# A decoder block on one core: another order of the seven-product steps in the feed-forward gate/up blocks, with the last one's raw weights split ahead of its sums

## The chip, the core and the metric

The kernel runs on one core of a Trainium2 chip. The metric is the time of one execution in device microseconds (us); less is better. The engines are TensorE (PE in the profile; PEld is its weight load), VectorE (DVE), ScalarE (ACT), GpSimd (POOL) and SyncE (SP), which here only issues DMAs.

## The reference

One layer of a decoder with 256 positions and a width of 2048: a normalised input goes through one wide projection, three groups of dilated window attention and a gated linear recurrence, whose outputs are mixed and added to the input. Then comes the feed-forward part, where the change is:

```python
a = rmsnorm(h, norm_ffn_pre[layer])
gt, up = jnp.split(a @ w_ffn_gate_up[layer], [D_FF], axis=-1)   # 2048 x (2 * 5632)
ff = (jax.nn.silu(gt) * up) @ w_ffn_down[layer]                 # 5632 x 2048
h = h + rmsnorm(ff, norm_ffn_post[layer])
```

All of it is float32.

## The kernel before

**Split numbers.** PE multiplies in a reduced 32-bit format (`F32R`). So each float32 weight tile is split on the fly: ACT copies it to the format (the high half, `w` or `dh`), and DVE subtracts that from the original (the low half, `wl` or `dl`). The activations are split in the same way, once. A product is then three matmuls: high by high, low weight by high activation, high weight by low activation.

**Blocks and steps.** Gate and up are computed in 11 blocks (0 to 10) of 512 gate and 512 up columns. A block has eight steps; a step `(m, kind)` takes rows 256m to 256m + 255 of the weights, as four tiles of 128 x 512. Two sides of 128 positions by two column groups by two row tiles make eight products, 24 matmuls of 512 columns. Kind 0 does just that ("plain"). Kinds 1 and 2 do the step in seven products, 21 matmuls, after a scheme like Strassen's: four of them need sums of weight tiles, and four sums of activations (`h7`). In kind 1 ("own sums") DVE makes the weight sums from the loaded tiles: three additions (`sum`, L476, L482, L483), ahead of the splits. In kind 2 ("fetched") the sums were made much earlier and stored in DRAM (`presum`); two DMAs fetch them (`s`), and only three of the four raw tiles are loaded beside. Either kind splits sums (`w` and `wl`, two halves of 1024 columns each) and three raw tiles (`dh` and `dl`, 1536 columns).

**Order of the products.** In `multiply_wide` a seven-product step takes the products with sums first and those with raw tiles behind, but in the last one of a block (`b.last7`) the raw ones first, so that the result bank `p1` is done early and `gather` can begin. Blocks 2 to 10 have the order `GATE_UP5`, block 1 `GATE_UP3`; in both, the step at place 6 is the block's last seven-product step. I number the places 0 to 7 and say "step 6" for them. In `GATE_UP5` before, the steps 2, 3 and 5 are fetched, 4 and 6 have own sums, and 0, 1 and 7 are plain.

**What sets the order on the engines.** There is no scheduler: each engine gets its instructions in the order in which the Python code issues them. During step i of PE, the code issues the split of step i + 2 (`prepare`), then DMAs on SP's queue: the sums for step i + 4 (`fetch_sums`) and the raw weights for step i + 5, which wait until the raw buffer of step i + 2 is free (three buffers). Between the steps stand the leftovers of the block before: `gather` (L553 to L557) and `complete` (L563) take its banks on DVE, ACT applies silu (L1460), DVE makes the product `e` (L1462). Then `turn_act` turns this product, which needs four DMA transposes on SP: ACT copies the words apart (L1413) behind the split of step 3, SP issues the transposes (L1419), and two steps on ACT copies the result together (L1428, it waits for the transposes) and sends it to DRAM (`acts`, L1430). Buffers for `dh` and `dl` serve two steps, so the split of step i waits until PE is through with that of two seven-product steps ago.

**Sums of activations.** `pair_sums` makes the five `h7` from `hT`, in pieces: at every `yield` the code goes on with other work, and it comes back twice per step.

Of the kernel before, what the change touches and what calls it, by code (L numbers as in the profile page):

```python
# [14 lines left out]
F32 = mybir.dt.float32  # L15
F32R = mybir.dt.float32r
I32 = mybir.dt.int32
U16 = mybir.dt.uint16
AF = mybir.ActivationFunctionType
# [23 lines left out]
    [(2, 0), (3, 0), (0, 1), (4, 0), (1, 1), (5, 0), (6, 0), (7, 0)],  # L43
]
GATE_UP3 = [(3, 0), (4, 0), (0, 2), (5, 0), (1, 1), (6, 0), (2, 2), (7, 0)]
GATE_UP5 = [(5, 0), (6, 0), (0, 2), (2, 2), (1, 1), (4, 2), (3, 1), (7, 0)]
PLACE = (0, 2, 1, 3)
DOWN = [[(m, m in by7) for m in range(KF // 2)] for by7 in (range(4, 20, 3), (2, 4, 7, 10, 13, 16, 18))]

# [53 lines left out]
def tile_hybrid_block(ctx: ExitStack, tc: tile.TileContext, t, out):  # L103
    nc = tc.nc
# [12 lines left out]
    def nm(s):  # L117
        serial[0] += 1
        return f"{s}_{serial[0]}"
# [13 lines left out]
    def p3(s, dtype, n, bufs, tag=None):  # L133
        return wide_pool[-1].tile([P, n], dtype, tag=tag or s, bufs=bufs, name=nm(s))
# [73 lines left out]
    def ptile(s):  # L208
        pool, n = (wide_pool[-1], 2) if wide_pool else (fp[0], 5)
        return pool.tile([P, 512], F32, tag="p", bufs=n, name=nm(s))  # L210
# [9 lines left out]
    blocks, chunks, wides, steps = [], [], [], []  # L220
# [27 lines left out]
    def add_wide_block(*args, **kw):  # L248
        b = Wide(*args, **kw)
        wides.append(b)  # L250
        for i in range(len(b.order)):
            n = len(steps)
            slots.append(lambda n=n: load_wide(n))
            items.append((steps, n, len(slots) - 1))
            steps.append([b, i, None, None])
# [39 lines left out]
    pre, pre_in = {}, {}  # L295
# [104 lines left out]
    def wslot():  # L400
        return stream.tile([P, 2048], F32R, tag="w", bufs=N_SPLIT, name=nm("w"))
# [41 lines left out]
    def split_wide(n):  # L443

        b, i, raw = steps[n][:3]
        m, by7 = b.order[i]
        prep = b.prep(m, by7) if b.prep else iter(())
        next(prep, None)
        if (b, i) == spare:
            hi = p3("spare", F32R, 2048, 1, "sum")  # L450
            lo = Joined(p3("spare", F32R, 1536, 4, "d"), p3("spare", F32R, 512, 4, "d"))
            nc.scalar.activation(hi, raw, AF.Copy)
            for c in (slice(0, 1536), slice(1536, 2048)):
                nc.vector.tensor_sub(lo[:, c], raw[:, c], hi[:, c].bitcast(F32))
            steps[n][3] = hi, lo
            return
        hi, lo = wslot(), p3("wl", F32R, 2048, 3)
        if not by7:
            for c in (slice(0, 1024), slice(1024, 2048)) if b.halves else (slice(0, 2048),):
                nc.scalar.activation(hi[:, c], raw[:, c], AF.Copy)  # L460
                next(prep, None)
                nc.vector.tensor_sub(lo[:, c], raw[:, c], hi[:, c].bitcast(F32))  # L462
            steps[n][3] = hi, lo
            return
        d = raw[:, 512:]
        if by7 == 2:
            for c, x in zip((slice(0, 1024), slice(1024, 2048)), pre_in.pop(n)):
                nc.scalar.activation(hi[:, c], x, AF.Copy)  # L468
                nc.vector.tensor_sub(lo[:, c], x, hi[:, c].bitcast(F32))  # L469
            dhi, dlo = p3("dh", F32R, 1536, 4, "d"), p3("dl", F32R, 1536, 4, "d")  # L470
            nc.scalar.activation(dhi, d, AF.Copy)
            nc.vector.tensor_sub(dlo, d, dhi.bitcast(F32))
            steps[n][3] = hi, lo, dhi, dlo
            return
        s = p3("sum", F32, 2048, 1)
        nc.vector.tensor_add(  # L476
            s[:, :1024].rearrange("p (a c) -> p a c", a=2),
            raw[:, 512:1536].rearrange("p (a c) -> p a c", a=2),
            raw[:, None, :512].to_broadcast([P, 2, 512]),
        )  # L480
        nc.scalar.activation(hi[:, :1024], s[:, :1024], AF.Copy)  # L481
        nc.vector.tensor_add(s[:, 1024:1536], raw[:, 512:1024], s[:, 512:1024])  # L482
        nc.vector.tensor_add(s[:, 1536:], raw[:, 1536:], s[:, 1024:1536])  # L483
        nc.scalar.activation(hi[:, 1024:], s[:, 1024:], AF.Copy)
        next(prep, None)
        dhi, dlo = p3("dh", F32R, 1536, 4, "d"), p3("dl", F32R, 1536, 4, "d")
        nc.scalar.activation(dhi, d, AF.Copy)  # L487
        for c in (slice(0, 1024), slice(1024, 2048)):
            nc.vector.tensor_sub(lo[:, c], s[:, c], hi[:, c].bitcast(F32))  # L489
        next(prep, None)  # L490
        nc.vector.tensor_sub(dlo, d, dhi.bitcast(F32))  # L491
        steps[n][3] = hi, lo, dhi, dlo

    def multiply_wide(n, sides=(0, 1), groups=(0, 1), between=lambda: None):
        b, i = steps[n][:2]
# [69 lines left out]
    def seven_sums(f, dst):  # L565

        s = ptile("s").rearrange("p (n t) -> p n t", n=4)
        a11, a12, a21, a22 = f[:, 0, :P], f[:, 1, :P], f[:, 0, P:], f[:, 1, P:]
        nc.vector.tensor_sub(s[:, 0, :], a22, a21)
        nc.vector.tensor_sub(s[:, 2, :], a11, a21)  # L570
        nc.vector.scalar_tensor_tensor(
            out=s[:, 1, :], in0=s[:, 0, :], scalar=-1.0, in1=a11, op0=OP.mult, op1=OP.subtract
        )
        nc.vector.tensor_add(s[:, 3, :], a12, s[:, 1, :])
        return (
            lambda: nc.scalar.activation(dst[:, 0], s, AF.Copy),
            lambda: nc.vector.tensor_sub(dst[:, 1], s, dst[:, 0].bitcast(F32)),
        )

    def sums_of(dst):  # L580
        return lambda n: (dst[:, 0, n, :], dst[:, 1, n, :])
# [3 lines left out]
    def pair_sums(src, out, slot, pairs=H7):  # L585

        for m in pairs:
            f = ptile("f").rearrange("p (k t) -> p k t", k=2)
            x = src.slots[m]
            nc.vector.tensor_add(f, x[:, :, 0, :].bitcast(F32), x[:, :, 1, :].bitcast(F32))  # L590
            dst = slot().rearrange("p (z n t) -> p z n t", z=2, n=4)
            yield
            for part in seven_sums(f, dst):
                yield
                part()
            out[m] = sums_of(dst)
            yield
# [216 lines left out]
    def more_x(c):  # L814
        if 0 < c < KD // 2 - 1:
            transpose_in(xt, colg, xT, c + 1)
        if c == 2:
            lanes[1].append(pair_sums(xT, x7, lambda: rslot("so")))
# [556 lines left out]
    def more_h(c):  # L1375
        if c + 1 < KD // 2:
            transpose_in(h_t, colg[:, 16:32], hT[0], c + 1)
        if c == 3:
            mix_gain(3, 1, wides[last_mix])
            residual_of(6, (0, 1), False)  # L1380
            residual_of(7, (0, 1), False)
            lanes[0].append(second_norm())
        if c == 4:
            lanes[1].append(pair_sums(hT[0], h7, lambda: rslot("so"), range(5)))
# [203 lines left out]
    def y_sums():  # L1588
        while not {0, 1} <= yT[0].there:
            yield  # L1590
        yield from pair_sums(yT[0], y7, lambda: rslot("so"), (0, 1))
# [27 lines left out]
    for half in range(2):  # L1619
        for g in range(3):  # L1620
            c = 1024 * g + 512 * half
# [28 lines left out]
    for j in range(1, 11):  # L1650
        add_wide_block(w, (512 * j, FF + 512 * j), GATE_UP5 if j > 1 else GATE_UP3, lambda k: hT[0](k),
                       lambda m: h7[m], evac_ffn, j % 2 == 0,
# [23 lines left out]
    for i in range(len(items)):  # L1676
        kind, n, _ = items[i]
        b, c = kind[n][:2]
# [99 lines left out]
```

## Time and profile before

| | before |
|---|---|
| median of 3 runs (lowest, highest) | 1692.96 us (1692.91, 1698.74) |
| the profiled execution | 1695.45 us, span of its instructions 1693.6 us |
| mean granted clock of TensorE | 0.998 |
| ACT: shares of the span, instructions | 59%, 1121 |
| DMA | 445.27 MB, mean 263 GB/s |
| gate/up blocks 1 to 10 | about 1040 to 1452 us of the span |

All times in the profile are counted from the start of the span. A row of the time line gives the start, the length, engine and line, what is written and read, and, in brackets, the idle time of the engine before it with what ended that. Lengths of rows that follow each other overlap by up to 0.1 us, so that the distance of two starts is the better measure of what an instruction costs on a full engine. The windows give the busy time of each engine in a stretch, the number of its instructions, the granted clock (1.00 is full speed), the DMA engines' share and GB/s.

### The profile page before, as it was taken

How to read it: one execution, taken by the hardware profiler on the slowest of the kernel's cores; microseconds unless marked ns; L12 is line 12 of the kernel's file. 1: busy time of each engine (PE TensorE's matmuls, PEld its weight loads, DVE VectorE, ACT ScalarE, POOL GpSimd, SP SyncE). 2: the span in 40 equal slices, each digit the busy share in tenths (PEclk: the TensorE clock that was granted, in tenths of full speed). 3: DMA queues.
4: the chain of work that ended last, by engine and by line, in shares of the span. 5: the costliest groups of instructions: out<-in, count | busy, mean ns of one | idle time of the engine just before them, and what ended most of it. 6: DMA issues, size and time to landing. Idle time of an engine off the chain costs nothing. (4 is left out here: it accounts for less than half of the span.)

```text
span 1693.6 us, 22264 instructions
## 1 busy us (share of the span) xinstructions
PE 1675.1 (99%) x8142; PEld 1401.8 (83%) x8142; DVE 1406.6 (83%) x1593; ACT 997.7 (59%) x1121; POOL 210.0 (12%) x358
## 2 busy tenths in 40 slices
PE   9999999999999999999999999999999999999997
PEld 7888888888888888888888888878888888788886
DVE  6999888866876876876578888999999999889987
ACT  6655555544455545555545557676777777665653
POOL 0012122234433432210000000000000000000000
PEclk9999999999999999999999999999999999999999
DMA  8578888899999999998868656998999999887673
GB/s 288 203 249 283 274 273 274 273 282 272 266 236 252 291 235 259 291 322 284 300 200 286 200 184 196 295 282 282 290 288 293 285 297 294 281 261 276 231 261 130
DMA packets 264640, 445.27 MB, mean 263 GB/s; under 512 B 39073, under 2 KB 105809, under 8 KB 263377
## 3 DMA queue, kind: packets, MB, share of 16 engines
q1 hardware_dynamic: 237936, 375.25, 68.4%
q0 software_dynamic: 17984, 41.97, 12.2%
q10 hardware_dynamic: 8608, 26.62, 4.2%
q8 instruction: 64, 1.05, 0.3%
q14 instruction: 48, 0.39, 0.1%
HBM read 414.41 MB, written 65.54 MB: 283 GB/s over the span
## 5 line engine op out<-in xcount | busy, mean ns | idle before, releaser
L140 PE MATMUL acc<-xT,w 128*128 128x256 f32 (+1 forms) x2048 | 365.1, 338 | 0.0
L140 PEld LDWEIGHTS acc<-xT,w 128*128 128x128 f32 x2048 | 312.0, 188 | 44.7
L462 DVE TENSOR_TENSOR wl<-raw,w 128x2048 fp32r<-128x2048 f32 (+1 forms) x131 | 284.0, 2175 | 62.8 <-ACT w L460 60.8
L407 DVE TENSOR_TENSOR w<-raw,w 128x1024 fp32r<-128x1024 f32 x176 | 215.3, 1223 | 144.0 <-ACT w L406 143.9
L406 ACT ACTIVATE w<-raw 128x1024 fp32r<-128x1024 f32 x176 | 186.1, 1059 | 192.7 <-PE acc L140 143.4
L460 ACT ACTIVATE w<-raw 128x2048 fp32r<-128x2048 f32 (+1 forms) x131 | 237.7, 1821 | 95.2 <-PE acc L140 23.0
L140 PE MATMUL acc<-w,xT 128*128 128x512 f32 x578 | 168.8, 392 | 0.0
L369 POOL COPY beats<-raw 128x1 f32<-128x1 f32 x185 | 103.7, 560 | 507.6 <-DMA raw<-in_w_in 506.7
L481 ACT ACTIVATE w<-sum 128x1024 fp32r<-128x1024 f32 x57 | 60.6, 1063 | 176.4 <-DVE sum L476 169.1
L489 DVE TENSOR_TENSOR wl<-sum,w 128x1024 fp32r<-128x1024 f32 x114 | 137.7, 1221 | 0.6 <-ACT w L481 0.6
L140 PE MATMUL acc<-w,hT 128*128 128x512 f32 x402 | 131.2, 392 | 0.4 <-DVE hT L1305 0.4
L140 PEld LDWEIGHTS acc<-w,xT 128*128 128x128 f32 x578 | 108.2, 188 | 22.2
L140 PE MATMUL aux<-w,xT 128*128 128x512 f32 x344 | 109.8, 389 | 0.0
L491 DVE TENSOR_TENSOR dl<-raw,dh 128x1536 fp32r<-128x1536 f32 x57 | 100.2, 1757 | 6.8 <-ACT dh L487 5.0
L140 PE MATMUL aux<-w,hT 128*128 128x512 f32 x318 | 102.8, 389 | 0.0
L140 PEld LDWEIGHTS acc<-w,hT 128*128 128x128 f32 x402 | 75.4, 188 | 16.3 <-DVE hT L1305 0.9
L140 PE MATMUL acc<-w,so 128*128 128x512 f32 x264 | 88.4, 389 | 0.0
L140 PE MATMUL acc<-w,a 128*128 128x512 f32 x268 | 83.8, 389 | 1.1 <-DVE e L563 1.1
L140 PE MATMUL aux<-w,so 128*128 128x512 f32 x252 | 84.4, 389 | 0.0
L487 ACT ACTIVATE dh<-raw 128x1536 fp32r<-128x1536 f32 x57 | 84.1, 1475 | 0.2 <-PE acc L140 0.2
L140 PE MATMUL aux<-w,a 128*128 128x512 f32 x254 | 79.4, 389 | 0.0
L469 DVE TENSOR_TENSOR wl<-s,w 128x1024 fp32r<-128x1024 f32 x58 | 68.3, 1220 | 12.2 <-ACT w L468 12.2
(293 smaller groups left out, 3261.1 us busy)
## 6 DMA issues: line engine op xcount, KB each, us to landing
raw<-in_w_in SPq DMA_DIRECT2D x270, 512.0 KB, 6.8
raw<-in_w_ffn_gate_up SPq DMA_DIRECT2D x147, 512.0 KB, 4.8
raw<-in_w_ffn_down SPq DMA_DIRECT2D x88, 512.0 KB, 5.8
presum<-in_w_ffn_gate_up POOLq DMA_DIRECT2D x120, 256.0 KB, 7.0
s<-presum SPq DMA_DIRECT2D x58, 512.0 KB, 7.1
raw<-in_w_mix_out SPq DMA_DIRECT2D x32, 512.0 KB, 4.9
act<-acts SPq DMA_DIRECT2D x22, 512.0 KB, 6.9
presum<-presum POOLq DMA_DIRECT2D x40, 256.0 KB, 6.5
```

The costliest lines, as they stand in the source:

```text
L140: nc.tensor.matmul(ps, lhsT, rhs, start=start, stop=stop, skip_group_check=True)
L369: nc.gpsimd.tensor_copy(beats, ahead[:, :1])
L406: nc.scalar.activation(wh, raw, AF.Copy)
L407: nc.vector.tensor_sub(wl, raw, wh.bitcast(F32))
L460: nc.scalar.activation(hi[:, c], raw[:, c], AF.Copy)
L462: nc.vector.tensor_sub(lo[:, c], raw[:, c], hi[:, c].bitcast(F32))
L469: nc.vector.tensor_sub(lo[:, c], x, hi[:, c].bitcast(F32))
L481: nc.scalar.activation(hi[:, :1024], s[:, :1024], AF.Copy)
L487: nc.scalar.activation(dhi, d, AF.Copy)
L489: nc.vector.tensor_sub(lo[:, c], s[:, c], hi[:, c].bitcast(F32))
L491: nc.vector.tensor_sub(dlo, d, dhi.bitcast(F32))
```

## The change

Three edits:

- `GATE_UP5`, the order of the steps in blocks 2 to 10: places 3 and 4 change kinds, as do 5 and 6. Now steps 2, 4 and 6 are fetched and 3 and 5 have own sums.
- In `split_wide`, for a fetched step that is the last seven-product step of its block (step 6 of blocks 1 to 10), the raw weights are split ahead of the sums. For all other steps the order stays; buffers for `dh` and `dl` are only named earlier.
- In `pair_sums`, the sums for m = 4 begin eight pieces (four steps) later. Only the list for `hT` has an m of 4.

```diff
-GATE_UP5 = [(5, 0), (6, 0), (0, 2), (2, 2), (1, 1), (4, 2), (3, 1), (7, 0)]
+GATE_UP5 = [(5, 0), (6, 0), (0, 2), (1, 1), (2, 2), (3, 1), (4, 2), (7, 0)]
...
         d = raw[:, 512:]
+        dhi, dlo = p3("dh", F32R, 1536, 4, "d"), p3("dl", F32R, 1536, 4, "d")
+        steps[n][3] = hi, lo, dhi, dlo
+        halves = slice(0, 1024), slice(1024, 2048)
+
+        def raw_high():
+            nc.scalar.activation(dhi, d, AF.Copy)
+
+        def raw_low():
+            nc.vector.tensor_sub(dlo, d, dhi.bitcast(F32))
+
         if by7 == 2:
-            for c, x in zip((slice(0, 1024), slice(1024, 2048)), pre_in.pop(n)):
+            if i == b.last7:
+                raw_high()
+                raw_low()
+            for c, x in zip(halves, pre_in.pop(n)):
                 nc.scalar.activation(hi[:, c], x, AF.Copy)
                 nc.vector.tensor_sub(lo[:, c], x, hi[:, c].bitcast(F32))
-            dhi, dlo = p3("dh", F32R, 1536, 4, "d"), p3("dl", F32R, 1536, 4, "d")
-            nc.scalar.activation(dhi, d, AF.Copy)
-            nc.vector.tensor_sub(dlo, d, dhi.bitcast(F32))
-            steps[n][3] = hi, lo, dhi, dlo
+            if i != b.last7:
+                raw_high()
+                raw_low()
             return
...
         for m in pairs:
+            for _ in range(8 if m == 4 else 0):
+                yield
             f = ptile("f").rearrange("p (k t) -> p k t", k=2)
```

What this does to the order of instructions is seen at three places. The changed kernel's lines have other numbers: L1413 is L1425 there, L1428 is L1440, the rows with `sum` are L488, L494 and L495.

On ACT, in block 5, from the copies that go before the transposes to the split of step 6. `w<-sum` and `w<-s` are high halves of own and of fetched sums, `dh<-raw` those of raw tiles; `e<-e` and `act<-e` are the two copies around the transposes. Before:

```order
L1413 ACTIVATE e_10164<-e_10165 128x1024 x2
L481 ACTIVATE w_10301<-sum_10303 128x1024
L484 ACTIVATE w_10301<-sum_10303 128x1024
L487 ACTIVATE dh_10309<-raw_10179 128x1536
L468 ACTIVATE w_10343<-s_10264 128x1024
L468 ACTIVATE w_10343<-s_10265 128x1024
L471 ACTIVATE dh_10349<-raw_10222 128x1536
L1428 ACTIVATE act_10377<-e_10165 128x1024 x2
L1430 DMA acts_10380<-act_10377 128x1024
L481 ACTIVATE w_10382<-sum_10384 128x1024
L484 ACTIVATE w_10382<-sum_10384 128x1024
L487 ACTIVATE dh_10390<-raw_10268 128x1536
```

Now, in the same place:

```order
L1425 ACTIVATE e_10164<-e_10165 128x1024 x2
L481 ACTIVATE w_10301<-s_10218 128x1024
L481 ACTIVATE w_10301<-s_10219 128x1024
L471 ACTIVATE dh_10303<-raw_10175 128x1536
L493 ACTIVATE w_10343<-sum_10347 128x1024
L496 ACTIVATE w_10343<-sum_10347 128x1024
L471 ACTIVATE dh_10345<-raw_10222 128x1536
L1440 ACTIVATE act_10381<-e_10165 128x1024 x2
L1442 DMA acts_10384<-act_10381 128x1024
L471 ACTIVATE dh_10388<-raw_10268 128x1536
L481 ACTIVATE w_10386<-s_10311 128x1024
L481 ACTIVATE w_10386<-s_10312 128x1024
```

Steps 4 and 5 have changed kinds, so that each pair of copies now stands behind a step with own sums and ahead of a fetched one; in step 6 `dh` has come to the front, right behind the second copies.

On SP's queue at the same place: raw weights for step 5 or 6, fetched sums, and the four transposes. Before:

```order
L290 DMA raw_10222<-in_w_ffn_gate_up 128x512
L290 DMA raw_10222<-in_w_ffn_gate_up 128x2x512
L363 DMA s_10264<-presum_4406 128x1024
L363 DMA s_10265<-presum_4406 128x1024
L290 DMA raw_10268<-in_w_ffn_gate_up 128x2x512 x2
L1419 DMA_TRANSPOSE e_10165<-e_10164 128x4x128 x4
L290 DMA raw_10315<-in_w_ffn_gate_up 128x2x512 x2
```

Now:

```order
L290 DMA raw_10222<-in_w_ffn_gate_up 128x2x512 x2
L290 DMA raw_10268<-in_w_ffn_gate_up 128x512
L290 DMA raw_10268<-in_w_ffn_gate_up 128x2x512
L1431 DMA_TRANSPOSE e_10165<-e_10164 128x4x128 x4
L363 DMA s_10311<-presum_4406 128x1024
L363 DMA s_10312<-presum_4406 128x1024
L290 DMA raw_10315<-in_w_ffn_gate_up 128x2x512 x2
```

The block's last fetched sums, for step 6 now and for step 5 before, have moved from ahead of the transposes to behind them.

On DVE, in block 2, from the end of step 2's split. Before, with step 3 a fetched one:

```order
L472 TENSOR_TENSOR dl_9271<-raw_9155,dh_9270 128x1536
L1462 TENSOR_TENSOR e_9217<-e_9217,e_9216 128x1024
L469 TENSOR_TENSOR wl_9307<-s_9227,w_9306 128x1024
L469 TENSOR_TENSOR wl_9307<-s_9228,w_9306 128x1024
L472 TENSOR_TENSOR dl_9313<-raw_9192,dh_9312 128x1536
```

Now; the rows with `hT` or `f` are the activation sums for m = 4, which stood in block 1 before (behind the split of its step 6):

```order
L474 TENSOR_TENSOR dl_9253<-raw_9147,dh_9252 128x1536
L602 TENSOR_TENSOR f_9281<-hT_8481 128x512
L1474 TENSOR_TENSOR e_9207<-e_9207,e_9206 128x1024
L579 TENSOR_TENSOR s_9299<-f_9281 128x128
L580 TENSOR_TENSOR s_9299<-f_9281 128x128
L581 SCALAR_TENSOR_TENSOR s_9299<-s_9299,f_9281 128x128
L584 TENSOR_TENSOR s_9299<-f_9281,s_9299 128x128
L488 TENSOR_TENSOR sum_9308<-raw_9182 128x1024
```

Five small instructions have come in between step 2's `dl` and step 3's own sums; before, the product `e` was followed at once by the `wl` of step 3.

More of the change, by code (lines that the diff above doesn't have):

```diff
@@ L485, in split_wide @@
         next(prep, None)
-        dhi, dlo = p3("dh", F32R, 1536, 4, "d"), p3("dl", F32R, 1536, 4, "d")
-        nc.scalar.activation(dhi, d, AF.Copy)
-        for c in (slice(0, 1024), slice(1024, 2048)):
+        raw_high()
+        for c in halves:
             nc.vector.tensor_sub(lo[:, c], s[:, c], hi[:, c].bitcast(F32))
         next(prep, None)
-        nc.vector.tensor_sub(dlo, d, dhi.bitcast(F32))
-        steps[n][3] = hi, lo, dhi, dlo
+        raw_low()
     def multiply_wide(n, sides=(0, 1), groups=(0, 1), between=lambda: None):
```

## The prediction

> **What bounds the kernel now.** I read the engine rows of the page, then who ends the waits of PE, then the gate/up blocks as windows from one `dl` of step 6 to the next, then the chain of waits for the pace of matmuls.
>
> ```profile
> PE 1675.1 (99%) x8142; PEld 1401.8 (83%) x8142; DVE 1406.6 (83%) x1593; ACT 997.7 (59%) x1121; POOL 210.0 (12%) x358
> ...
> PE acc L140 <- DVE dl L491: 2.9, 5, 1.3
> PE aux L140 <- DVE dl L491: 1.3, 4, 0.5
> PE acc L140 <- ACT dh L487: 0.5, 1, 0.5
> ...
> 1112.72:1155.01 42.29, 42.04 (x177) 34.34 (x177) 38.31 (x33) 29.11 (x25) 0.00 (x0) 0.96 0.93 280
> 1196.09:1236.77 40.68, 40.43 (x177) 33.14 (x177) 38.13 (x33) 29.02 (x25) 0.00 (x0) 1.00 0.95 291
> sum 327.96, PE 325.02 PEld 266.36 DVE 305.17 ACT 232.85 POOL 0.00; mean PE 40.63 PEld 33.30 DVE 38.15 ACT 29.11 POOL 0.00
> ...
> 1510.71 12.92 PE acc L140 x57
> ```
>
> PE sets the time (99% busy). Unhindered it takes 12.92 / 57 = 0.2267 us for a matmul, and a gate/up block has 177 of them: 40.13 us. Eight blocks take 327.96 us, 40.99 each. What is missing is the wait rows (from 1105 to 1445 us): in each of the nine blocks 2 to 10 PE waits once for `dl` of L491, the low half of the raw weights of step 6, and in block 2 for its `dh` too. If the change takes all of these away, eight blocks give 327.96 - 8 x 40.13 = 6.9 us and block 2 some 2.2 (1.3 and 0.5 idle, with the refill of the array behind each wait): 9 us, 0.5%. That is all that there is to win.
>
> The windows say what speaks against it. DVE is busy 38.13 of a block's 40.68 us. It may stand idle 40.13 - 38.13 = 2.0 us per block; beyond that DVE paces the loop and not PE. So I followed DVE and ACT through block 5.
>
> ```profile
> 1196.12 4.50 DVE L462 TENSOR_TENSOR wl<-raw,w 128x2048 fp32r<-128x2048 f32 x2
> ...
> 1205.50 2.48 DVE L563 TENSOR_TENSOR e<-acc,e 128x512 f32<-128x512 f32 x4
> 1209.13 2.36 DVE L469 TENSOR_TENSOR wl<-s,w 128x1024 fp32r<-128x1024 f32 x2 [1.15 <-ACT w L468]
> 1211.45 1.76 DVE L472 TENSOR_TENSOR dl<-raw,dh 128x1536 fp32r<-128x1536 f32 x1
> 1213.13 1.22 DVE L1462 TENSOR_TENSOR e<-e,e 128x1024 f32<-128x1024 f32 x1
> 1214.26 2.36 DVE L469 TENSOR_TENSOR wl<-s,w 128x1024 fp32r<-128x1024 f32 x2
> ...
> 1218.20 1.22 DVE L476 TENSOR_TENSOR sum<-raw 128x1024 f32<-128x1024 f32 x1
> ...
> 1225.07 2.36 DVE L469 TENSOR_TENSOR wl<-s,w 128x1024 fp32r<-128x1024 f32 x2
> 1228.15 1.76 DVE L472 TENSOR_TENSOR dl<-raw,dh 128x1536 fp32r<-128x1536 f32 x1 [0.73 <-ACT dh L471]
> 1229.83 1.22 DVE L476 TENSOR_TENSOR sum<-raw 128x1024 f32<-128x1024 f32 x1
> ...
> 1236.80 4.49 DVE L462 TENSOR_TENSOR wl<-raw,w 128x2048 fp32r<-128x2048 f32 x2
> ...
> 1207.42 0.72 ACT L1460 ACTIVATE e<-e,r2c 128x512 f32<-128x512 f32 x1 [0.47 <-DVE e L563]
> 1208.05 1.99 ACT L468 ACTIVATE w<-s 128x1024 fp32r<-128x1024 f32 x2
> 1209.95 1.47 ACT L471 ACTIVATE dh<-raw 128x1536 fp32r<-128x1536 f32 x1
> ...
> 1213.85 1.48 ACT L471 ACTIVATE dh<-raw 128x1536 fp32r<-128x1536 f32 x1
> 1215.23 1.99 ACT L1413 ACTIVATE e<-e 128x1024 uint16<-128x1024 uint16 x2
> 1219.52 1.06 ACT L481 ACTIVATE w<-sum 128x1024 fp32r<-128x1024 f32 x1 [2.29 <-DVE sum L476]
> ...
> 1221.88 1.48 ACT L487 ACTIVATE dh<-raw 128x1536 fp32r<-128x1536 f32 x1
> ...
> 1226.62 1.49 ACT L471 ACTIVATE dh<-raw 128x1536 fp32r<-128x1536 f32 x1 [1.37 <-PE acc L140]
> 1228.02 2.58 ACT L1428 ACTIVATE act<-e 128x1024 uint16<-128x1024 uint16 x2
> 1230.63 0.33 ACTq L1430 DMA_DIRECT2D acts<-act  x1
> ...
> 1218.32 0.90 SPq L290 DMA_DIRECT2D raw<-in_w_ffn_gate_up  x2
> 1219.31 6.43 SPq L1419 DMA_TRANSPOSE e<-e  x4
> ...
> 1236.81 0.50 PE L140 MATMUL aux<-dl,hT 128*128 128x512 f32 x1 [0.25 <-DVE dl L491]
> ```
>
> From these starts DVE's round is: steps 7, 0, 1 with the last block's sums 13.01 (1196.12 to 1209.13, 1.15 of it idle); step 2 and the product `e` 5.13; step 3, fetched, 3.94; step 4, own sums, 6.87; step 5, fetched, 4.76 (0.73 idle, because its `dh` needs a buffer that PE frees); step 6, own sums, 6.97. Sum 40.68, the window. In the left-out stretch 1196 to 1209 no DVE row but the one at 1209.13 shows an idle time over 0.1: there is no slack in which a late step would be made up. Note also where ACT's two copies for the turned activations stand: L1413 behind fetched step 3, when DVE still has a `dl` and then a sum from raw weights to do, L1428 behind fetched step 5, when DVE has step 6's sums to do. DVE does not feel either.
>
> **The change, part by part.** Numbers of instructions and bytes stay; only places change.
>
> *New order, steps 3 to 5.* DVE's work is the same 38.13. Step 3 with own sums starts where the fetched one did, 1214.26, and takes 6.87: to 1221.13. In step 4 of before, ACT's `dh` starts 3.68 after the sum (1218.20 to 1221.88), so now at 1217.94. Behind it stand the L1413 copies: 1.38 later (1213.85 to 1215.23), 1219.32 to 1221.31. Only then comes fetched step 4's first `w<-s`, 1.05 long (half of the 1.99 pair): 1222.3. DVE, free at 1221.13, waits **1.2 us**. Step 4 then takes 2.32 + 1.68 = 4.0 (1209.13 to 1211.45 to 1213.13), to 1226.3; step 5, own sums, 6.87, to 1233.2, with its `dh` on ACT from 1230.0 to 1231.5. The 0.73 wait for PE goes: that `dh` needs step 3 out of PE, at 1226.6 by the row of before.
>
> *Raw ahead of sums in step 6.* `dh` of step 6 is now ACT's first instruction of the step and stands behind the L1428 copies and the issue of `acts`: 1231.4 + 2.6 (1228.02 to 1230.63) + 0.33 = 1234.4, ended 1235.85. DVE has nothing ahead of `dl` in its queue and waits from 1233.2 to 1235.9, **2.7 us**; behind `dl` are queued this step's two `wl` and all of steps 7, 0, 1. `dl` ends at 1237.6, later than the 1236.77 at which it freed PE. That PE needs the sums 2.0 us (nine matmuls) after `dh` helps nothing where `dl` itself is later. With 1.68 for `dl` and 2.32 for the two `wl`, step 7's `wl` starts at 1239.87 where it was 1236.80.
>
> So DVE's round is 13.01 + 5.13 + 6.87 + 1.19 + 4.0 + 6.87 + 2.68 + 4.0 = **43.75 us** (1239.87 - 1196.12), against PE's 40.13. Nothing in it waits for PE, so it repeats at its own pace: eight blocks 350.0, less 327.96, is **+22.0 us**. PE loses 3.6 us per block, in steps 5 and 6.
>
> All this rests on DVE and ACT not passing over an instruction that waits. The rows show it: the product `e` (L1462) had its last input from ACT at 1208.14 (1207.42 + 0.72), but DVE stood idle until 1209.13 for the `wl` ahead of it and made the product at 1213.13. If the two could pass, the copies would cost nothing and the first rival below would hold, 1684 us instead of the sum. The Trainium skill, "TensorE: Matmul & The Clock Gate", Part 1, "Architectural detail", says the same as a rule: ScalarE and VectorE serve their queues strictly in order, and only TensorE pulls weight loads forward. By that rule the copies hold `dh` back, and the trace agrees, with 1.0 us of idle DVE in front of a ready product.
>
> *Queue of SP.* Raw weights of step 6 wait for step 3's `dl`, 2.9 later than 1218.32, and the four transposes stand behind: issue from 1222.2. Before, they had landed at the latest when L1428 began unhindered, 1228.02, 8.7 after their first issue; now by 1230.9, just ahead of 1231.4. I take 0; bounds -0 (they can't help) to +1 per block. The fetched sums of step 6 are issued behind the transposes, at 1228.7; ACT wants them at 1235.8, 7.1 later, against a median of 7.1 to landing (row below). I take 0, as the transposes' queue is then empty; the bound is +1 per block, +8.
>
> *Fifth activation sums.* They leave a stretch of block 1 that waits for a transfer anyway and come into block 2, between step 2 and step 3.
>
> ```profile
> s<-presum SPq DMA_DIRECT2D x58, 512.0 KB, 7.1
> ...
> 1070.17 0.69 DVE L590 TENSOR_TENSOR f<-hT 128x512 f32<-128x512 f32 x1
> 1070.89 0.29 DVE L569 TENSOR_TENSOR s<-f 128x128 f32<-128x128 f32 x1
> ...
> 1085.90 2.36 DVE L469 TENSOR_TENSOR wl<-s,w 128x1024 fp32r<-128x1024 f32 x2 [1.15 <-ACT w L468]
> ...
> 1071.95 0.63 ACT L576 ACTIVATE so<-s 128x512 fp32r<-128x512 f32 x1 [0.78 <-DVE s L574]
> ...
> 1438.91 1.76 DVE L491 TENSOR_TENSOR dl<-raw,dh 128x1536 fp32r<-128x1536 f32 x1
> ...
> 1452.13 0.47 PE L140 MATMUL acc<-w,a 128*128 128x512 f32 x1 [1.14 <-DVE e L563]
> ```
>
> On DVE 0.7 + four of 0.24 (1070.89 to the next row at 1071.83) = 1.65, on ACT 0.55 ahead of the L1413 copies. Block 2 from 1085.90: 5.13 + 1.65 + 6.87 + 1.2 + 0.55 + 4.0 + 6.87 + 2.7 = 1114.9, and `dl` ends at 1116.6, against 1112.72 (the first window's start): **+3.9 us**. Its late `low` part (L577) fills the 1.7 gap. Block 1's step 6 is also raw-first now, but PE does not wait there (no such wait before 1105); 0, between 0 and +0.5.
>
> *Into the down projection.* PE starts it when DVE has taken block 10's banks: 13.22 after the start of step 6's `dl` (1438.91 to 1452.13). Now two `wl` stand between: 15.5. **+2.3 us.** PE idles some 3.6 there.
>
> In block 2 the clock fell right behind 1.8 us of idle PE: granted 0.96 in the window that begins there, that is (1 - 0.96) x 42.29 / 0.5 = 3.4 us at half, 1.7 us of work lost. With PE waiting 3.6 per block this may happen in many blocks; there it costs nothing, since PE has 3.6 to spare and DVE takes the banks (L563) only 9.4 after step 7's `wl` starts (1196.12 to 1205.50). At the start of the down projection it can cost 0 to 1.7; I take **+1**.
>
> Sum: 22.0 + 3.9 + 2.3 + 1 = +29.2 us, on the profiled execution's 1695.45 (span 1693.6): 1724.7. That execution is 2.5 above the median of the runs, 1692.96; on the median it is 1722.2, so **1722 us**.
>
> **The rivals.**
> - *It does what it says*: DVE is not held by the copies, `dl` of step 6 is there in time, PE runs at 40.13. Then -9: 1684. For it: `dl` comes two `wl` (2.3) earlier within its step. It decides if DVE's idle time stays under 2.0 per block; I count 1.15 + 1.2 + 2.7 and some 0.6 of small ones (40.68 - 38.13 - 1.15 - 0.73). Chance 0.09.
> - *The lateness is made up in each block*: steps 7, 0, 1 hold slack that these rows hide, and each block loses only what `dl` is later by itself, 0.8, and the down projection 2.3: 9 x 0.8 + 2.3 = +9.5, 1702. Against: DVE's rows from 1196 to 1209. Chance 0.10.
> - *More than that*: transposes and fetched sums land late as well, +1 in each block, or the halved clock adds its 1.7: 1722 + 9 to 15, 1731 to 1737. Chance 0.07.
>
> **How the numbers follow.** The forecast has 0.74, with a range of its own of 1712 to 1729: each of the two new waits by 0.5 per block one way or the other. 1700 to 1732 adds the made-up case and part of the last; outside stay the first rival and the far end, under 0.2. No change is within 0.5%, 8.5 us, about what this measurement can tell. Faster: the first rival, 0.09. The made-up case lies on the edge: half of it, and little else, is "same", 0.06. The rest is slower, 0.85.
>
> **What would show it.** Windows from `dl` to `dl` of step 6 near 43.75 with DVE busy 38.1 and PE idle; on DVE a wait of 1.2 for `w<-s` in step 4 and of 2.7 for `dh` in step 6; on ACT the copies between; PE's waits in steps 5 and 6, for `wl` and `dl`, of some 3 us in sum. I am wrong if the windows are at 40.1: then ACT gets `dh` out ahead of what I think, or DVE had slack that I didn't see.

## The result, and the profile after

| | before | changed |
|---|---|---|
| median (lowest, highest), 4 runs each | 1694.33 us (1692.91, 1698.74) | 1735.51 us (1733.18, 1736.12) |
| the profiled execution, its span | 1695.45 us, 1693.6 us | 1735.01 us, 1733.2 us |
| mean granted clock of TensorE | 0.998 | 0.992 |

The change makes the kernel slower: the ratio of the changed kernel to the one before is 1.0236, 95% interval 1.0213 to 1.0259. The forecast, 1722 us in a range of 1700 to 1732, had the direction and most of the mechanism. It was 13.5 us too low, and the time lies 3.5 above the range.

The busy time of each engine on the page of the changed kernel:

```profile
PE 1688.9 (97%) x8142; PEld 1406.8 (81%) x8142; DVE 1408.0 (81%) x1593; ACT 995.8 (57%) x1121; POOL 201.4 (12%) x358
```

Its windows from the end of `dl` of step 6 in one block to that of the next: the first, one in the middle, the last, and the sum of the eight.

```profile
1115.50:1160.07 44.57, 42.56 (x178) 34.20 (x177) 38.27 (x35) 28.86 (x26) 0.00 (x0) 0.96 0.81 265
1340.04:1384.72 44.68, 41.31 (x177) 32.98 (x177) 38.26 (x35) 28.85 (x26) 0.00 (x0) 1.00 0.79 263
1429.49:1474.21 44.72, 42.68 (x178) 34.23 (x177) 38.25 (x34) 28.86 (x26) 0.00 (x0) 0.96 0.85 268
sum 358.71, PE 336.11 PEld 268.76 DVE 306.21 ACT 231.05 POOL 0.00; mean PE 42.01 PEld 33.60 DVE 38.28 ACT 28.88 POOL 0.00
```

Who ended PE's and DVE's waits in these eight rounds (total us, times, longest us):

```profile
PE acc L140 <- DVE wl L500: 4.7, 7, 0.8
PE acc L140 <- ACT w L496: 4.6, 4, 1.2
PE aux L140 <- ACT w L496: 4.5, 4, 1.1
PE aux L140 <- DVE wl L500: 3.4, 6, 0.8
PE acc L140 <- DVE dl L474: 2.6, 2, 1.3
PE aux L140 <- DVE dl L474: 2.5, 2, 1.3
...
DVE dl L474 <- ACT dh L471: 19.3, 11, 2.7
DVE wl L482 <- ACT w L481: 17.8, 16, 1.1
DVE wl L462 <- ACT w L460: 7.9, 8, 1.6
DVE dl L474 <- DMA raw<-in_w_ffn_gate_up: 5.6, 2, 3.0
```

DVE's work is the same, 38.28 us per round against 38.15 before. A round is 44.84 us long (358.71 / 8), not 40.99, because DVE now waits in three places: for `dh` of step 6, once in each of the eight rounds and 2.66 to 2.96 us long (the first and the last DVE row together; they also hold the same wait in block 2, 2.7 us, just ahead of the first round, and four short waits of 0.15 in other steps; two of the long ones are put down to a DMA that had landed 9 us earlier), twice per round for `w` of fetched sums (1.14 in step 2, as before, and 1.09 in step 4, which is new), and for `w` of L460, the high half of a plain step's raw weights (7.9 in all). PE waits 22.3 us in the eight rounds, 2.8 per round: for own sums, those of step 5 above all (`w` of L496, `wl` of L500), and for `dl`.

The round from 1338 to 1383 us as DVE, ACT and SP's queue went through it (rows of the time line; idle time before a row in brackets):

```profile
1338.29 1.76 DVE L474 TENSOR_TENSOR dl<-raw,dh 128x1536 fp32r<-128x1536 f32 x1 [2.67 <-ACT dh L471]
...
1342.23 2.28 DVE L462 TENSOR_TENSOR wl<-raw,w 128x2048 fp32r<-128x2048 f32 x1
1345.40 2.29 DVE L462 TENSOR_TENSOR wl<-raw,w 128x2048 fp32r<-128x2048 f32 x1 [0.88 <-ACT w L460]
...
1356.20 2.36 DVE L482 TENSOR_TENSOR wl<-s,w 128x1024 fp32r<-128x1024 f32 x2 [1.14 <-ACT w L481]
...
1361.34 1.22 DVE L488 TENSOR_TENSOR sum<-raw 128x1024 f32<-128x1024 f32 x1
...
1366.52 1.76 DVE L474 TENSOR_TENSOR dl<-raw,dh 128x1536 fp32r<-128x1536 f32 x1
1369.36 2.36 DVE L482 TENSOR_TENSOR wl<-s,w 128x1024 fp32r<-128x1024 f32 x2 [1.09 <-ACT w L481]
...
1373.37 1.22 DVE L488 TENSOR_TENSOR sum<-raw 128x1024 f32<-128x1024 f32 x1
...
1382.97 1.76 DVE L474 TENSOR_TENSOR dl<-raw,dh 128x1536 fp32r<-128x1536 f32 x1 [2.67 <-ACT dh L471]
...
1343.45 1.92 ACT L460 ACTIVATE w<-raw 128x2048 fp32r<-128x2048 f32 x1 [1.50 <-DMA raw<-in_w_ffn_gate_up]
...
1366.39 1.99 ACT L1425 ACTIVATE e<-e 128x1024 uint16<-128x1024 uint16 x2
1368.29 1.99 ACT L481 ACTIVATE w<-s 128x1024 fp32r<-128x1024 f32 x2
...
1377.03 1.47 ACT L471 ACTIVATE dh<-raw 128x1536 fp32r<-128x1536 f32 x1
1378.41 2.56 ACT L1440 ACTIVATE act<-e 128x1024 uint16<-128x1024 uint16 x2
...
1381.45 1.49 ACT L471 ACTIVATE dh<-raw 128x1536 fp32r<-128x1536 f32 x1 [0.48 <-DMA raw<-in_w_ffn_gate_up]
...
1330.11 0.82 SPq L363 DMA_DIRECT2D s<-presum  x2
1335.64 9.72 SPq L290 DMA_DIRECT2D raw<-in_w_ffn_gate_up  x6
```

ACT stands as forecast: both copies of L1425 lie ahead of step 4's `w`, both of L1440 and the issue of `acts` ahead of step 6's `dh`, with no gap in which ACT could have started earlier (the 0.48 before `dh` is the issue of `acts`). New is the row at 1345.40: step 0 of the next block comes 0.88 late to DVE, since ACT stood idle until its raw weights were there (1343.45, idle 1.50). They were issued at 1335.64, as soon as `dl` of step 5 had freed their buffer (1335.61). Below are the raw weights issued at that point, with their median time to landing: first of the changed kernel, then of the kernel before at the same point of block 5.

```profile
raw<-in_w_ffn_gate_up SPq DMA_DIRECT2D x2, 512.0 KB, 6.5
```

```profile
raw<-in_w_ffn_gate_up SPq DMA_DIRECT2D x2, 512.0 KB, 5.3
```

Counted from the end of step 5's `dl`, the later half of these weights landed 7.9 us after it in the mean of the eight rounds, 6.6 before. DVE wants its subtraction for step 0 some 9.0 after it (9.1 before), and ACT's split needs 1.9 of that. So there were 7.1 us, and the weights took 7.9. All of the 7.9 us at L462 is this step 0.

### The profile page after: what moved, and what is told of

It reads as the page before. It is cut to its first block, busy times and chain, and to the rows that moved or that the text cites. A ratio compares the mean times of both kernels' runs of the same rounds, so it can differ in the third digit from the quotient of the medians.

```text
span 1733.2 us, 22255 instructions
## 1 busy us (share of the span) xinstructions
PE 1688.9 (97%) x8142; PEld 1406.8 (81%) x8142; DVE 1408.0 (81%) x1593; ACT 995.8 (57%) x1121; POOL 201.4 (12%) x358
## 3 DMA queue, kind: packets, MB, share of 16 engines
q0 software_dynamic: 17984, 41.97, 12.2%
q8 instruction: 64, 1.05, 0.3%
## 5 line engine op out<-in xcount | busy, mean ns | idle before, releaser
L462 DVE TENSOR_TENSOR wl<-raw,w 128x2048 fp32r<-128x2048 f32 (+1 forms) x131 | 284.6, 2175 | 74.4 <-ACT w L460 72.7
L460 ACT ACTIVATE w<-raw 128x2048 fp32r<-128x2048 f32 (+1 forms) x131 | 238.3, 1822 | 101.2 <-PE acc L140 24.3
L474 DVE TENSOR_TENSOR dl<-raw,dh 128x1536 fp32r<-128x1536 f32 x86 | 151.1, 1757 | 33.3 <-ACT dh L471 23.7
L369 POOL COPY beats<-raw 128x1 f32<-128x1 f32 x185 | 94.7, 512 | 515.2 <-DMA raw<-in_w_in 514.0
L500 DVE TENSOR_TENSOR wl<-sum,w 128x1024 fp32r<-128x1024 f32 x114 | 137.8, 1221 | 0.0
L471 ACT ACTIVATE dh<-raw 128x1536 fp32r<-128x1536 f32 x86 | 126.8, 1474 | 5.1 <-DMA raw<-in_w_ffn_gate_up 2.9
L140 PE MATMUL aux<-w,so 128*128 128x512 f32 x252 | 87.9, 403 | 5.8 <-ACT w L496 5.8
L140 PEld LDWEIGHTS acc<-w,hT 128*128 128x128 f32 x402 | 76.2, 190 | 16.7 <-DVE hT L1317 0.9
```

Source lines behind the costliest of these rows:

```text
L140: nc.tensor.matmul(ps, lhsT, rhs, start=start, stop=stop, skip_group_check=True)
L369: nc.gpsimd.tensor_copy(beats, ahead[:, :1])
```

## The experiments

Ratios are to the kernel before, run beside each kernel on the same chip (1697.05, 1696.68 or 1697.29 us there; the forecast's base was 1692.96). "Round" is the mean of the eight, from `dl` to `dl` of step 6; its parts for each kernel are in a table behind the last experiment. Where an expectation names theories by letters, A is the mechanism of the prediction (queues in order, and the place of ACT's copies), E says that SP's queue makes the late raw weights, F that the release of their buffer does; the others are rivals of the run at which they stand. A row of waits has the total in us, how many, and the longest.

**1. The order, with the sums ahead in step 6 as elsewhere.** Of the changed kernel, the raw-first split alone is undone; if it makes the cost, this returns to the time before.

```diff
         if by7 == 2:
-            if i == b.last7:
-                raw_high()
-                raw_low()
             for c, x in zip(halves, pre_in.pop(n)):
...
-            if i != b.last7:
-                raw_high()
-                raw_low()
+            raw_high()
+            raw_low()
```

> The changed kernel without the raw-first split: step 6 splits its sums first again; the new order and the late activation sums stay. Theory A (ACT's two pairs of copies for the turned activations stand ahead of a fetched step's splits, and DVE, which serves in order, paces the round): the second pair now holds up the first w<-s of step 6 (1.05 us) where it held up dh (1.48), so DVE's wait of 2.67 in step 6 becomes 2.25, for wl and not for dl; a round is 0.4 shorter than the changed kernel's 44.8, and the time is 1731 us, 1727 to 1735. Theory B (splitting raw ahead of sums is what costs): the time falls back to that of before, 1694, or under it.

1736.53 us, ratio 1.0233 (1.0215 to 1.0250): as slow as the change itself. DVE's waits in its eight rounds:

```profile
DVE wl L479 <- ACT w L478: 35.5, 24, 2.4
DVE wl L462 <- ACT w L460: 12.4, 11, 1.6
```

Step 6 now waits for its first `w` instead of for `dh`: 2.17 in seven of the eight rounds and not 2.67, as ACT's first instruction behind the copies is a half of 1.05 us and not a `dh` of 1.48. That gives back 4 us, which are lost again at L462, where the waits grow from 7.9 to 12.4. Step 0's raw weights land when they did (7.8 after step 5's `dl`) and are now wanted 0.3 earlier: 10.0 of the 12.4. The other 2.4 are three waits in step 1, and not for raw weights. The longest of them, as ACT saw it:

```profile
1261.56 1.92 ACT L460 ACTIVATE w<-raw 128x2048 fp32r<-128x2048 f32 x1 [3.30 <-PE aux L140]
```

The weights had landed at 1260.1; ACT began when PE was through with step 6, since there are three buffers for `w` and step 1 takes that of step 6. So the raw-first split is not the cost, and B falls: the 0.5 that step 6 gains without it is lost behind it. A had the shorter wait in step 6 (2.25) but not the longer ones behind it, and its range of 1727 to 1735 was missed by 1.5 us (the kernel before took 2.7 more beside this run than beside the result).

**2. The old order, with the two other edits kept.** With the old `GATE_UP5`, step 6 of blocks 2 to 10 has own sums, so raw-first acts in block 1 alone.

```diff
-GATE_UP5 = [(5, 0), (6, 0), (0, 2), (1, 1), (2, 2), (3, 1), (4, 2), (7, 0)]
+GATE_UP5 = [(5, 0), (6, 0), (0, 2), (2, 2), (1, 1), (4, 2), (3, 1), (7, 0)]
```

> The changed kernel with the old order of steps in blocks 2 to 10: what is left of the change is raw-first in block 1 and the late activation sums. Theory A: only block 2 gets longer, by the 1.65 us of DVE and 0.55 of ACT that move into it: 1694 + 2 = 1696 us, 1694 to 1698; rounds of 40.7 in blocks 3 to 10. Rival C (the late sums or raw-first in block 1 cost a good part of the 41 us): over 1702.

1699.97 us, ratio 1.0016 (1.0005 to 1.0027): by the ratio, 2.7 us above before. That is 2 us over the 1694 to 1698 expected (on the same slower base), and its rounds are 41.15 and not 40.7; rival C falls. Nearly all of the cost comes with the order.

**3. The turned activations one step earlier.** In the changed kernel, ACT's copies are moved ahead by one step: L1425 then stands behind fetched step 2, L1440 behind fetched step 4, both ahead of own sums, for which ACT has time.

```diff
-                       pre=begin_wides if j == 1 else None, turn=1)
+                       pre=begin_wides if j == 1 else None, turn=0 if j > 1 else 1)
```

> The changed kernel, but in blocks 2 to 10 the product is turned one step earlier: the first copies stand ahead of step 3's own sums, the second ahead of step 5's own sums, where ACT waits 3 to 4 us for DVE's sum anyway. Same work, same bytes. Theory A: DVE's wait of 1.09 in step 4 falls to nothing with at most 0.5 in step 3 in its place, that of 2.67 in step 6 goes; rounds of 40.3 to 41.5 and a time of 1690 to 1708 us. Rival D (DVE's work with two own-sum steps before a raw-first step, or late transfers, make the round long, wherever the copies stand): 1725 or more.

1711.23 us, ratio 1.0081 (1.0066 to 1.0096): two thirds of the loss are gone, a little less than the mechanism gave (up to 1708 us and 41.5 per round); the rival that the copies' place does not matter falls. The waits in steps 4 and 6 have disappeared; 0.49 remains per round in step 3. But the round is 42.31, because the waits for raw weights at L462 have doubled, to 16.7 (12.3 in step 0, 4.4 in step 7): without the 2.7 in step 6, DVE wants step 0's weights 6.1 to 7.3 us after step 5's `dl` and no longer 9.0. The copies' place is the main cost; a second one was behind it, and grows when the first goes.

**4. The same copies, in the old order.** If that is so, moving the second copies later in the kernel before, behind step 6's own sums, must cost by itself. This adds one step to their delay; the order of the steps is untouched.

```diff
         yield
         yield
+        if now[0].order is GATE_UP5:
+            yield
         x = rslot("act").bitcast(F32)
```

> The kernel before with its order of steps and splits; only the second pair of copies for the turned activations (2.6 us, and 0.3 for the DMA's issue) goes one step later in blocks 2 to 10: from ahead of step 6's own sums to behind them, ahead of step 7's w<-raw. Theory A (a pair of copies costs where ACT's next split is what DVE needs next): DVE waits some 3.0 us for w<-raw in step 7, rounds of 42.9, 18 to 24 us more, ratio 1.010 to 1.014. Theory G (it is the order of the steps, with own sums ahead of fetched ones, that costs): ratio under 1.003.

1714.32 us, ratio 1.0098 (1.0076 to 1.0120), just under the 1.010 to 1.014 that the mechanism gives; the round is 42.87, where 42.9 was expected. ACT and DVE at one of the eight places, in step 6 and on into step 7:

```profile
1239.17 1.47 ACT L487 ACTIVATE dh<-raw 128x1536 fp32r<-128x1536 f32 x1
1240.55 2.53 ACT L1430 ACTIVATE act<-e 128x1024 uint16<-128x1024 uint16 x2
...
1243.54 3.71 ACT L460 ACTIVATE w<-raw 128x2048 fp32r<-128x2048 f32 x2 [0.46 <-ACT act L1430]
...
1240.67 1.76 DVE L491 TENSOR_TENSOR dl<-raw,dh 128x1536 fp32r<-128x1536 f32 x1
1245.48 4.49 DVE L462 TENSOR_TENSOR wl<-raw,w 128x2048 fp32r<-128x2048 f32 x2 [3.05 <-ACT w L460]
```

Three microseconds of ACT work between `dh` of own sums and the next step's `w` become three microseconds of idle DVE, eight times over (24.4 in all). The round grows by 1.9 of them, since other waits of DVE are gone that the kernel before had (4.4 for `dh` in step 5 and 3.1 at L462 in eight rounds). This shows the mechanism without the new order, against the rival G.

**5. The last fetched sums ahead of the transposes.** On SP's queue the change moved step 6's sums behind the four transposes. Here they are issued one step earlier, ahead of them; the rest is the changed kernel.

```diff
         fetch_sums(i + AHEAD + 2)
+        if i + AHEAD + 3 < len(items) and items[i + AHEAD + 3][0] is steps:
+            b, c = steps[items[i + AHEAD + 3][1]][:2]
+            if b.order is GATE_UP5 and c == 6:
+                fetch_sums(i + AHEAD + 3)
```

> The changed kernel, but the two DMAs of step 6's fetched sums are issued one step earlier, ahead of the four transposes on SP's queue. This is about the part that the prediction missed: 1.0 us per round of DVE waiting for w<-raw in step 0, whose raw weights land 7.3 to 7.7 us after their issue. Theory E (the fetched sums behind the transposes crowd these weights): that wait goes, rounds of 43.8, 1727 us. Theory F (the weights are issued too late, because own-sum step 5 frees their buffer with its last instruction): no change, 1735 within 2.

1726.42 us, ratio 1.0172 (1.0157 to 1.0187). The waits in steps 4 and 6 stay, those at L462 (L466 in this kernel and in experiments 6 to 8) fall from 7.9 to 2.2, and the round from 44.84 to 44.06. The raw weights issued at the point shown above for the changed kernel, in the same block:

```profile
raw<-in_w_ffn_gate_up SPq DMA_DIRECT2D x2, 512.0 KB, 5.6
```

Step 0's raw weights are still issued when step 5's `dl` frees the buffer, but land 7.1 after it (mean of eight) and not 7.9. In the changed kernel the sums were issued just ahead (1330.11), and step 7's raw weights behind them. When step 0's were issued, the second half of the sums and all of step 7's weights were still on their way: they landed at 1336.7, 1338.1 and 1339.5. The sums themselves are in time either way. So where they stand among SP's DMAs costs, as E had it, 0.8 us per round, through the weights behind them.

**6. Both, 3 and 5.**

> The two last edits together: the changed kernel, the product turned one step earlier and step 6's fetched sums issued one step earlier. With the turn alone DVE's waits for the copies were gone (0.49 left in step 3), but 2.1 us per round of waiting for step 7's and step 0's raw weights had come up; with the sums alone that wait was 0.3. Theory A with E: both are gone, DVE idles 1.15 + 0.5 + some 0.7, rounds of 40.4 to 40.9, as before: a ratio of 0.996 to 1.003 to before. Rival (the raw weights are late because the transposes now stand ahead of step 6's weights, whatever the sums do): rounds of 42, ratio over 1.006.

1707.03 us, ratio 1.0057 (1.0036 to 1.0078). That is above the range expected (0.996 to 1.003): the round is 41.65, and the plain steps still wait 11.7. The rival's 1.006 lies in the interval, so this run leaves open what makes the weights late. DVE with the copies out of the way, at the end of one block:

```profile
1320.58 3.43 DVE L478 TENSOR_TENSOR dl<-raw,dh 128x1536 fp32r<-128x1536 f32 x2
...
1326.19 2.28 DVE L466 TENSOR_TENSOR wl<-raw,w 128x2048 fp32r<-128x2048 f32 x1
1329.62 2.29 DVE L466 TENSOR_TENSOR wl<-raw,w 128x2048 fp32r<-128x2048 f32 x1 [1.14 <-ACT w L464]
```

The first row holds `dl` of steps 5 and 6, back to back. `dl` of step 5, done at some 1322.25, frees the buffer into which step 0's weights of the next block go; DVE wants their low half at 1328.4, 6.2 us later. In the kernel before, `dl` of step 5 is done at 1229.8 and the same `wl` begins at 1239.0, 9.2 later, because a step with three additions and all of its subtractions lies between. ACT's split takes 1.9 of it, which leaves 4.3 us and 7.3. The weights land 5.6 after the release in the mean of this kernel, 6.6 in the kernel before: late in every round here, in one of the eight there.

**7. As 6, with the fifth activation sums in their old place.**

```diff
         for m in pairs:
-            for _ in range(8 if m == 4 else 0):
-                yield
```

> As the kernel with both edits (turn one step earlier, sums ahead), and the fifth activation sums are not late, but in block 1 as before. Theory A: block 2 loses 1.65 us of DVE and 0.55 of ACT; 1 to 3 us less than with late sums. Rival: they are hidden in block 2, no difference over 1 us.

1704.46 us, ratio 1.0042 (1.0026 to 1.0059), 2.6 below experiment 6. The two intervals overlap, so this alone does not settle what the late sums cost; with the 2.7 of experiment 2 it agrees.

**8. As 7, with an earlier release.** If the release of the buffer sets the wait, splitting the raw weights of steps 3 and 5 between the two halves of the sums, and not behind them, must take most of it away.

```diff
+        if b.order is GATE_UP5:
+            raw_high()
+            nc.scalar.activation(hi[:, 1024:], s[:, 1024:], AF.Copy)
+            nc.vector.tensor_sub(lo[:, :1024], s[:, :1024], hi[:, :1024].bitcast(F32))
+            raw_low()
+            nc.vector.tensor_sub(lo[:, 1024:], s[:, 1024:], hi[:, 1024:].bitcast(F32))
+            return
```

> The new order with the turn one step earlier, step 6's sums ahead and no late activation sums, and in the own-sum steps 3 and 5 the raw weights are split between the two halves of the sums, so that their buffer is free 1.2 us earlier. There 1.5 us per round of waiting for raw weights was left in steps 7 and 0. Theory F (with own-sum step 5 right ahead of the short fetched step 6, the weights of step 0 can't be asked for early enough; DVE needs them 6 us after dl of step 5, and ACT 2 before that): 1.2 earlier takes most of it, 0.3 to 0.6 left, rounds of 40.5 to 40.9, ratio 0.998 to 1.002. Rival H (traffic on the DMA queues sets the landing, not the time of issue): rounds stay at 41.5, ratio 1.003 or more.

1698.29 us, ratio 1.0008 (0.9999 to 1.0018). The waits for raw weights fall from 12.2 to 3.3; where experiment 6 waited, the two `wl` now follow each other (the last row is ACT's, for the wait in the first):

```profile
1317.65 1.76 DVE L478 TENSOR_TENSOR dl<-raw,dh 128x1536 fp32r<-128x1536 f32 x1 [0.61 <-ACT dh L475]
...
1321.60 4.49 DVE L466 TENSOR_TENSOR wl<-raw,w 128x2048 fp32r<-128x2048 f32 x2
...
1316.13 1.49 ACT L475 ACTIVATE dh<-raw 128x1536 fp32r<-128x1536 f32 x1 [1.07 <-PE acc L140]
```

F holds for the waits that experiment 5 had left, 0.4 per round, and for the time. It does not hold for the round: 41.38 is nearer to H's 41.5 than to the 40.5 to 40.9 of F. One round of 44.53, in which step 0's weights land 8.7 after the release, weighs in it (the other seven take 40.93 in the mean), and in step 6 DVE now waits 7.1 in all for a `dh` whose buffer PE has not freed, so that PE's pace counts again. The two profiled executions, of experiments 7 and 8, differ by 9.9 us, and of these 2.3 are in the eight rounds and 5.8 at the start of the down projection and behind it. As a whole the new order is now as fast as the old one. What it cost was the copies, the queue and the release, one behind the other.

**9 and 10. The kernel before, with the raw weights split between the sums.** The wait that the change set out from, PE for `dl` of step 6, can also be shortened in the old order. Number 9 does it in step 6 alone (by `i == b.last7`), number 10 in steps 4 and 6:

```diff
+        if b.order is GATE_UP5:
+            nc.scalar.activation(dhi, d, AF.Copy)
+            nc.scalar.activation(hi[:, 1024:], s[:, 1024:], AF.Copy)
+            nc.vector.tensor_sub(lo[:, :1024], s[:, :1024], hi[:, :1024].bitcast(F32))
+            nc.vector.tensor_sub(dlo, d, dhi.bitcast(F32))
+            nc.vector.tensor_sub(lo[:, 1024:], s[:, 1024:], hi[:, 1024:].bitcast(F32))
+            steps[n][3] = hi, lo, dhi, dlo
+            return
```

> The kernel before, its order kept, but in the own sums of step 6 the raw weights are split between the two halves of the sums: on ACT first half, dh, second half, on DVE wl, dl, wl. So dl ends 1.2 us earlier and nothing new stands in front of it. Theory A: PE's wait for dl (0.25 to 0.66 and 0.11 of refill in each of nine blocks, 1.8 with the halved clock in block 2) goes, rounds of 40.2 to 40.4 and 5 to 9 us less: ratio 0.995 to 0.997. Rival (DVE's round of 40.7 is at its own pace before too, and PE then waits elsewhere): ratio 0.999 or more.

> The kernel before, with the raw weights split between the halves of the sums in both own-sum steps, 4 and 6, and not in 6 alone (which gave 0.9965). Step 4's raw buffer is free 1.2 us earlier, and with it step 7's weights, on which nothing waited for long: ratio 0.995 to 0.998, the same as with step 6 alone. Rival: ACT's second half of step 4's sums, now behind dh, holds up DVE: over 0.999.

Number 9 takes 1691.36 us, ratio 0.9965 (0.9952 to 0.9978), in the range expected. Its round is not: 40.62, where 40.2 to 40.4 was expected, and of the 4.5 us that PE waited in eight rounds, 3.0 are left, for `dl`. Two of its rounds take 42.2; in both ACT's second copies waited over 2 us for the transposes (2.8 and 2.2), and DVE 1.9 behind them. Number 10 takes 1689.78 us, ratio 0.9957 (0.9943 to 0.9970), and is the fastest kernel here. PE's waits in the eight rounds of number 10, where before had 2.7, 1.3 and 0.5:

```profile
PE aux L140 <- DVE dl L489: 1.0, 1, 1.0
PE acc L140 <- DVE dl L489: 0.7, 1, 0.7
```

The two intervals overlap: what step 4 adds is not settled.

Waits of DVE per round, the mean or the span of the eight; for the plain steps the sum of the eight:

| kernel | round | step 6 waits | step 4 waits | plain steps wait for `w` (sum of 8 rounds) | ratio |
|---|---|---|---|---|---|
| before | 40.99 | 0 to 0.44 | 0.15 to 0.49 | 3.1 | 1 |
| changed | 44.84 | 2.70 | 1.09 | 7.9 | 1.0236 |
| 1 sums ahead in step 6 | 45.14 | 2.21 | 1.08 | 12.4 | 1.0233 |
| 2 old order | 41.15 | 0 to 2.00 | 0.15 to 0.49 | 2.8 | 1.0016 |
| 3 copies earlier | 42.31 | 0 | 0 (0.49 in step 3) | 16.7 | 1.0081 |
| 5 sums ahead of transposes | 44.06 | 2.66 | 1.08 | 2.2 | 1.0172 |
| 6 = 3 + 5 | 41.65 | 0 to 0.13 | 0 (0.49 in step 3) | 11.7 | 1.0057 |
| 7 = 6, early activation sums | 41.67 | 0 | 0 (0.50 in step 3) | 12.2 | 1.0042 |
| 8 = 7, earlier release | 41.38 | 0.50 to 1.86 | 0 (0.50 in step 3) | 3.3 | 1.0008 |
| 4 before, copies later | 42.87 | 0.15 | 0.15 | 24.4 (step 7, for the copies) | 1.0098 |
| 9 before, earlier `dl` in step 6 | 40.62 | 0 to 1.93 | 0.15 | 1.5 | 0.9965 |
| 10 before, the same in steps 4 and 6 | 40.51 | 0 to 1.27 | 0 to 0.75 | 3.5 | 0.9957 |

## Why the prediction was right or wrong

*What bounds the kernel, and that DVE would pace it.* Right. PE's waits for `dl` were worth little, and beyond 2.0 us of idle time per block DVE sets the round. PE's 2.8 us of waits per round answer to the forecast's "some 3".

*The terms of the round*, from the starts between 1338.29 and 1382.97 above:

| term | forecast | measured | rows |
|---|---|---|---|
| steps 7, 0, 1 | 13.01 | 13.97 | 1342.23 to 1356.20 |
| step 2 and `e` | 5.13 | 5.14 | to 1361.34 |
| step 3, own sums | 6.87 | 6.93 | to the end of `dl`, 1368.27 |
| wait for `w<-s`, step 4 | 1.19 | 1.09 | bracket at 1369.36 |
| step 4 | 4.0 | 4.01 | to 1373.37 |
| step 5, own sums | 6.87 | 6.93 | to 1380.30 |
| wait for `dh`, step 6 | 2.68 | 2.67 | bracket at 1382.97 |
| step 6 | 4.0 | 3.94 | 1338.29 to 1342.23 |
| sum | 43.75 | 44.68 | |

Both new waits came out within 0.1 us. They could be worked out that closely because each was a chain of starts on one engine that serves its queue in order, and experiment 4 shows the same chain by itself.

*The step that failed* is the first term, "steps 7, 0, 1" as an unchanged 13.01, together with the one that fed it: "*Queue of SP* ... I take 0". Over the eight rounds the forecast was 350.0 and the trace shows 358.71; of the 8.7 missing, 7.9 are DVE's waits at L462 for raw weights of plain steps. There are two faults in it:
- The base was block 5, a round of 40.68 in which no raw weights were late, while the eight rounds of before average 40.99 and hold three waits at L462, 3.1 us. Two of them, 2.0 us, are for raw weights that landed late; in the third ACT waited for PE. The 22.0 was a difference between a clean round and an average one. The row of before for its eight rounds:

```profile
DVE wl L462 <- ACT w L460: 3.1, 3, 1.1
```

- I asked of SP's queue only whether the moved DMAs themselves come in time. They do: L1440 begins at 1378.41 right behind `dh`, and no `w<-s` of step 6 waits. What came behind the moved DMAs, the raw weights of steps 7 and 0, I did not follow. Experiment 5 takes the sums from ahead of them, and L462's 7.9 becomes 2.2.

*Block 2 and the fifth activation sums*: forecast +3.9; `dl` of step 6 ended at 1115.50 instead of 1112.72, **+2.8**. Block 2 began 1 us earlier than before (1084.91 instead of 1085.90, at the `wl` of its step 2), so that the block itself lost 3.8. Right for the block. That the change made block 2 begin earlier is not shown: experiment 4, whose code is that of before up to there, came to the same place at 1087.02.

*Into the down projection*: forecast 15.5 from the start of `dl` to the first matmul, 2.3 more than before. It was 17.56 (1472.46 to 1490.02), **+4.3**. DVE and PE there:

```profile
1472.46 1.76 DVE L474 TENSOR_TENSOR dl<-raw,dh 128x1536 fp32r<-128x1536 f32 x1 [2.66 <-ACT dh L471]
...
1481.40 2.29 DVE L462 TENSOR_TENSOR wl<-raw,w 128x2048 fp32r<-128x2048 f32 x1 [2.11 <-ACT w L460]
...
1490.02 0.77 PE L140 MATMUL acc<-w,a 128*128 128x512 f32 x1 [5.44 <-DVE e L573]
```

The two `wl` of step 6 are there, as forecast, and another 2.11 for raw weights of the down projection: the same term left out once more. PE idles 5.4, where 3.6 was forecast.

*The halved clock*: **+1.7** behind the transition where +1 was taken; the first 5 us there were granted 0.50, in the kernel before 1.00. Inside the blocks nothing, as argued: rounds with a granted clock of 0.96 (44.57 to 44.77) are no longer than those at 1.00 (44.53 to 45.62).

The sum: 2.8 + 30.8 (358.71 - 327.96) + 4.3 + 1.7 = 39.6, the difference of the two spans, against a forecast of 29.2. Of the 10.4 missing, 8.7 are in the rounds, 2.0 at the transition and 0.7 behind it, less 1.1 in block 2. The rival "more than that", 1731 to 1737, had the time, but by luck: it had transposes and fetched sums land late; these came in time, and the raw weights behind them did not. "It does what it says" and "made up in each block" are ruled out by the windows: DVE's rounds hold no slack, as the rows from 1196 to 1209 had shown.

## What to carry to other kernels

Where two in-order engines split the work, a lump on one of them (here 2 to 3 us of copies) is free only ahead of a step in which the other has enough to do by itself; changing the kinds of the steps moves the lump without touching it. When a DMA moves on a queue, follow what stands behind it to its consumer, and when the work between the release of a buffer and its next use shrinks, compare that time with the transfer's. Take a base for "unchanged" stretches from the mean of all rounds, not from the cleanest one.

## What the runs showed of the hardware

Two short waits of PE can be followed by half its clock. PE's rows in step 5 of block 3, and a window right behind them with its granted clock (third column from the end):

```profile
1152.54 0.49 PE L140 MATMUL acc<-w,so 128*128 128x512 f32 x1 [1.16 <-ACT w L496]
1153.80 0.50 PE L140 MATMUL acc<-wl,so 128*128 128x512 f32 x1 [0.77 <-DVE wl L500]
```

```profile
1154.45:1157.87 3.42, 3.42 (x10) 2.69 (x9) 1.20 (x1) 2.94 (x3) 0.00 (x0) 0.51 1.05 357
```

The same two waits of PE in block 7:

```profile
1332.50 0.50 PE L140 MATMUL acc<-w,so 128*128 128x512 f32 x1 [1.14 <-ACT w L496]
1333.76 0.50 PE L140 MATMUL acc<-wl,so 128*128 128x512 f32 x1 [0.76 <-DVE wl L500]
```

Two waits of 1.16 and 0.77 us, with one matmul between them, were followed by 3.4 us at half clock (0.51); nearly the same pair in a later round, 1.14 and 0.76, was not (that round was granted 1.00). Of the nine blocks 2 to 10 of the changed kernel, five show the half clock behind this pair. The Trainium skill, "TensorE: Matmul & The Clock Gate", "Why this matters for your kernels", advises to have no gaps of over some 3 us. Here two waits that come to 1.9 us were followed by half clock in some blocks and not in others. Their length alone does not decide it: in experiment 5 a pair of 0.87 and 0.77 (1284.7 us) was followed by half clock, one of 1.16 and 0.76 (1417.3 us) was not. What does decide it is open.
